# One lasting PSUM tile for attention scores and transposes, with two sets of columns for the transposes

## The chip, the cores and the metric

The kernel runs on one core of a Trainium2 chip. The metric is the device time of one execution in microseconds (us); the kernel before was run three times. One further execution was recorded by the hardware profiler, and all traces here come from such executions. PE is the matmul engine (PEld its weight loads), DVE the vector engine, ACT the scalar engine, POOL the general one, and SP issues DMAs.

## The reference

One layer of a hybrid encoder on a sequence of 2048 tokens of width 1024: an RMS norm feeds one input projection; half of its outputs go through a diagonal complex state-space scan (SSM) with a gated unit, the other half through chunked attention; both are normalised, joined by an output projection and a residual, and followed by a SwiGLU feed-forward block and a last norm. The part that matters here, cut:

```python
# 8 heads of 64; a chunk of 64 queries sees its own and the 8 previous chunks (BAND = 576 keys)
scores = jnp.einsum('bnqhd,bnkhd->bhnqk', qc, kb) / math.sqrt(HEAD_DIM)
scores = scores + bias[None, :, None, :, :]
scores = jnp.where(valid[None, None, :, None, :], scores, -1e30)
probs = jax.nn.softmax(scores, axis=-1)
out = jnp.einsum('bhnqk,bnkhd->bnqhd', probs.astype(v.dtype), vb)
```

## The kernel before

The kernel writes fp32 products as sums of two or three products of rounded parts: a `hi` part (a copy by ACT) and a `lo` part (the rest, by DVE). Matmul operands come from SBUF; results go to PSUM, of which a partition has eight pieces (banks) of 512 fp32 columns.

`att_phase` (about 130 to 740 us of the profiled execution) walks through 128 steps. A step is one block of 512 tokens (`sb`, four of them), one pair of heads (`pr`, four), one head of the pair (`hh`) and one group of 128 queries (`qp`, four). In step `s` the kernel emits, in the order `"sptf"`:

- **s, `scores(s)`**: the scores of 128 queries against `nk` keys, 640 in blocks 1 to 3, and 128, 256, 384 and 512 in the first block. They are the matmuls `sc<-k,q2h` and `sc<-k,q2l` (L79, a helper that records all matmuls), into the tile `sc` of two banks. 640 keys are done as 2 x 320 columns, one half in each bank. Then DVE adds the bias and takes the minimum in one pass (L849, two rows in the trace: the pass `s<-sc` and the read-out of the minimum, `mn`), and ACT does the exponential (L852, `s<-s,mn`).
- **p, `pv_head` and `pv_scale`**: every fourth step the product of a finished head's probabilities with v (16 matmuls `pj<-pth,v` and `pj<-ptl,v`, 8 in the first block), and every eighth step four transposes that spread the softmax sums.
- **t, `transp(s - 2)`**: up to five 128 x 128 transposes of the exponentials of two steps earlier (L82, `pt<-ident,s`) into the tile `pt` (five blocks of 128 columns, two banks); then ACT copies them to `pth` (L867) and DVE writes the rest to `ptl` (L868).
- **f**: the fillers, which are slices of other work spread over the steps by `Unit`: projections of later blocks (`pf`), v, and the SSM groups (`pj<-U,Bst` and others), whose scan POOL does.

With `PINA` set, all of these matmuls and transposes are kept in program order on PE. A scheduler orders the other engines and derives the semaphore waits from the accesses to each tile. `sc` and `pt` are allocated anew in every step, each with one buffer, so the next step's tile waits until the readers of the last one are through. PSUM in this phase holds two banks for `pf`, two for `pj`, two for `pt` and two for `sc`. From step 119 on the SSM buffers are given back and the mixing phase (the gated unit, then the output projection) begins among the last steps; after it come the feed-forward phases, which the change does not touch.

Of the kernel before, what the change touches and what calls it, by code (L numbers as in the profile page):

```python
# [13 lines left out]
ALU = mybir.AluOpType  # L14
AX = mybir.AxisListType

P = 128
# [9 lines left out]
SB = 512  # L27
# [69 lines left out]
def f32(ap):  # L97
    return ap.bitcast(F32)
# [302 lines left out]
def u_phase(k, ident, S, aw):  # L401
# [3 lines left out]
    with ExitStack() as cx:  # L405
# [113 lines left out]
        for n in range(1, NSB):  # L519
            last, b = BLOCKS[n - 1 : n + 1]  # L520
            prep(b)
            if n == 1:
                bias_corners(k, S["nba"])
                bias_rows(k, S, 0, S["nba"])
            pf = FBANKS[n]
            now = [group(b, 0, 0 in pf)]
            finish(last, held)
            long(1)
            if n == NSB - 1:
                att = att_phase(k, ident, S, aw, X[b], lambda: ST[b])  # L530
                next(att)
            for f in (1, 2):
                now.append(group(b, f, f in pf))
                if n > 1:
                    long(1)
            sums(b)
            held = now + [group(b, 3, 3 in pf)]
# [140 lines left out]
def att_phase(k, ident, S, aw, x0, roots):  # L678

    tc, nc, io, pfs = k.tc, k.nc, k.io, k.pfs  # L680
    with ExitStack() as cx:
# [138 lines left out]
        def load_nb(h):  # L820
            return bias_rows(k, S, h, nbt[h % 2])

        def scores(st):
            sb, pr, hh, qp = st
            h = 2 * pr + hh
            if qp == 0:
                hd = st_head[sb, h] = Head()
                hd.nb = nbs.pop(h) if nbs else load_nb(h)
                hd.s = {}
                hd.p = None  # L830
            hd = st_head[sb, h]
            if qp == 2 and (sb, h) < (NSB - 1, H - 1):
                nbs[(h + 1) % H] = load_nb((h + 1) % H)
            q2h, q2l, k2 = qk[sb, pr][hh]
            k0 = max(qp, 4) if sb == 0 else qp
            nk = (qp + 5 - k0) * P
            half = nk // 2 if nk > 512 else nk
            nch = nk // half
            ps = k.t(psum2, "sc", [P, 2, 512])
            for c in range(nch):  # L840
                c0 = k0 * P + c * half + k2.shape[1] - 2 * SB
                cols = slice(c0, c0 + half)
                for n, q2 in ((0, q2h), (1, q2l)):
                    k.ta.matmul(ps[:, c, :half], q2[:, qp * P : (qp + 1) * P], k2[:, cols], start=n == 0, stop=n == 1)
            s = k.t(aa, "s", [P, 640], bufs=3)
            mn = k.t(aa, "mn", [P, 1], bufs=4)
            if (hh, qp) == (0, 0):
                sums[sb, pr] = k.t(aa, "sm", [P, 2, 4], bufs=3)
            nc.vector.tensor_tensor_reduce(  # L849
                s[:, :nk].rearrange("p (a b) -> p a b", a=nch), ps[:, :nch, :half],  # L850
                hd.nb[:, nk - 1 :: -1].rearrange("p (a b) -> p a b", a=nch), 1.0, 3e38, ALU.add, ALU.min, mn[:])
            nc.scalar.activation(s[:, :nk], s[:, :nk], AF.Exp, bias=mn[:], scale=-1.0, accum_out=sums[sb, pr][:, hh, qp : qp + 1])  # L852
            hd.s[qp] = s, k0

        def transp(st):
            sb, pr, hh, qp = st
            hd = st_head[sb, 2 * pr + hh]
            if qp == 0:
                hd.p = k.t(aa, "pth", [P, 5, 4, P], F32R), k.t(aa, "ptl", [P, 5, 4, P], F32R)
            pth, ptl = hd.p  # L860
            s, k0 = hd.s.pop(qp)
            pt = k.t(psum, "pt", [P, 5, P], bufs=1)
            for kb in range(k0, qp + 5):
                k.ta.transpose(pt[:, kb % 5, :], s[:, (kb - k0) * P : (kb - k0 + 1) * P], ident[:])
            runs = [(0, 5)] if sb else ([(4, 5)] if qp == 0 else [(4, 5), (0, qp)])
            for a, b in runs:
                nc.scalar.copy(pth[:, a:b, qp, :], pt[:, a:b, :])  # L867
                nc.vector.tensor_tensor(ptl[:, a:b, qp, :], pt[:, a:b, :], f32(pth[:, a:b, qp, :]), op=ALU.subtract)  # L868
# [54 lines left out]
        sp = tc.alloc_tile_pool(name="ssm", reuse_waits="tile", bufs=1)  # L923
        psum = cx.enter_context(tc.tile_pool(name="aps", bufs=1, space=bass.MemoryType.PSUM, reuse_waits="tile"))
        psum2 = cx.enter_context(tc.tile_pool(name="aps2", bufs=1, space=bass.MemoryType.PSUM, reuse_waits="tile"))
        units = []
        for sb in range(NSB):
            g0 = sb * 32
# [12 lines left out]
        for s in range(N + LAG + 2):  # L941
            if s == OPEN:
                aw.release()
                mix = mix_phase(k, S, lambda: k.t(pfs, "pf", [P, 512]))
                units += [Unit(islice(mix, MIX_N), MIX_N, GSTART, N + LAG, GSTART - OPEN)]
            if s == GSTART:
                sp.release()
            for o in ORDER:
                if o == "s" and s < N:
                    scores(steps[s])  # L950
                elif o == "t" and LAG <= s < N + LAG:
                    transp(steps[s - LAG])
                elif o == "p" and LAG + 1 <= s < N + LAG + 1 and steps[s - LAG - 1][3] == 3:
                    pv_head(steps[s - LAG - 1])
                elif o == "p" and s >= LAG + 2 and steps[s - LAG - 2][2:] == (1, 3):
                    pv_scale(steps[s - LAG - 2])
                elif o == "f":
                    for u in units:
                        u.advance(s)
# [737 lines left out]
```

## Time and profile before

| | |
|---|---|
| runs | 2290.89, 2288.25, 2294.39 us; median 2290.89 |
| profiled execution | 2289.1 us, span 2287.1 us |
| PE busy | 2171.6 us (95%), 10632 matmuls and transposes |
| DVE, ACT, POOL busy | 1544.7 (68%), 1000.6 (44%), 348.7 us (15%) |
| granted PE clock, mean | 0.978 |

Busy time is the time in which an engine had an instruction under way. A row of the trace names the line, the engine, the operation, the tile written and those read, and their shapes. A releaser (`<-`) is the instruction whose semaphore ended an engine's idle time. Matmul ends are modelled.

### The profile page before, as it was taken

What the parts mean: (1) busy time and instruction counts of PE and PEld (TensorE: products, weight loads), DVE (VectorE), ACT (ScalarE), POOL (GpSimd) and SP (SyncE); (2) the same over time, 40 slices, a digit from 0 to 9 for tenths busy, and PEclk for the clock granted to TensorE, in tenths of its full rate; (3) what the DMA queues carried; (4) which work ended last, traced back from release to release, by engine and by line L of the source; (5) the groups of instructions that cost most, each with busy time, mean ns of one, the idle gap of its engine ahead of it and who ended that gap; (6) DMA issues with size and microseconds to landing.
All of it is one profiled execution on the core that took longest, in us unless ns stands there. A gap on an engine that the chain in (4) does not pass through costs nothing.

```text
span 2287.1 us, 30278 instructions
## 1 busy us (share of the span) xinstructions
PE 2171.6 (95%) x10632; PEld 1830.1 (80%) x10632; DVE 1544.7 (68%) x2695; ACT 1000.6 (44%) x1654; POOL 348.7 (15%) x813
## 2 busy tenths in 40 slices
PE   8988899999996899999999999999999989999997
PEld 6777688898985788878888887888888778888886
DVE  7755565555556766876776678666666477789776
ACT  6444555455557652343333335333333343344322
POOL 2245765455660000000000000000000000000000
PEclk9998999999998999999999999999999999999999
DMA  8767886666644534854465567555423297465552
GB/s 299 236 221 220 257 223 201 187 188 179 188 132 124 171 121 147 267 189 151 160 200 178 167 211 258 203 169 188 139 96 110 78 341 252 166 212 193 206 189 74
DMA packets 215256, 428.33 MB, mean 187 GB/s; under 512 B 38592, under 2 KB 61168, under 8 KB 208000
## 3 DMA queue, kind: packets, MB, share of 16 engines
q1 hardware_dynamic: 210368, 412.50, 55.3%
q0 software_dynamic: 4736, 13.91, 2.0%
q8 instruction: 83, 1.36, 0.2%
q14 instruction: 69, 0.57, 0.1%
HBM read 286.86 MB, written 129.00 MB: 182 GB/s over the span
## 4 chain that ended last, share of the span: by engine, by line
PE 80%; DVE 6%; DMA 4%; POOL 4%; issue 3%; ACT 1%; SPq 1%; DVEq 0%; POOLq 0%; ACTq 0%
PE X L79 20%; PE ps L79 19%; PE Y L79 10%; PE pf L79 9%; PE big L79 9%; PE W L79 5%; PE pj L79 4%; PE sc L79 2%; PE pt L82 2%; DMA xt<-in_xp 1%; DMA hd<-wc 1%; POOL X L605 1%; DVE lo L156 1%; POOL X L604 1%; POOL st L602 1%
## 5 line engine op out<-in xcount | busy, mean ns | idle before, releaser
L79 PE MATMUL X<-hi,c 128*128 128x512 f32 x1408 | 451.0, 391 | 6.9 <-DVE c L156 5.4
L79 PE MATMUL ps<-hd,hd 128*128 128x512 f32 (+1 forms) x1968 | 430.8, 381 | 6.1 <-ACT hd L156 4.5
L79 PEld LDWEIGHTS ps<-hd,hd 128*128 128x128 f32 x1968 | 358.0, 189 | 77.7 <-ACT hd L156 5.3
L79 PEld LDWEIGHTS X<-hi,c 128*128 128x128 f32 x1408 | 265.3, 189 | 63.4 <-DVE c L156 6.3
L79 PE MATMUL X<-lo,c 128*128 128x512 f32 x704 | 274.9, 391 | 0.0
L156 ACT CAST hd<-hd 128x1536 fp32r<-128x1536 f32 (+1 forms) x106 | 147.7, 1393 | 236.3 <-DMA hd<-hq 178.7
L79 PE MATMUL Y<-hi,c 128*128 128x512 f32 x704 | 224.7, 390 | 1.5 <-DVE u L1389 1.5
L156 DVE TENSOR_TENSOR hd<-hd 128x1536 fp32r<-128x1536 f32 (+1 forms) x106 | 174.4, 1646 | 29.1 <-ACT hd L156 28.4
L156 DVE TENSOR_TENSOR c<-S,c 128x512 fp32r<-128x512 f32 x176 | 121.0, 689 | 98.3 <-ACT c L156 98.0
L1385 ACT COPY u<-X 128x512 f32<-128x512 f32 x132 | 77.4, 587 | 200.7 <-PE X L79 200.7
L1513 DVE TENSOR_TENSOR acc<-acc,ps 128x512 f32<-128x512 f32 x196 | 130.9, 684 | 50.3 <-PE ps L79 47.8
L156 ACT CAST c<-S 128x512 fp32r<-128x512 f32 x176 | 109.4, 622 | 120.1 <-PE Y L79 61.6
L79 PE MATMUL pf<-hi,w 128*128 128x512 f32 x416 | 153.9, 422 | 8.4 <-ACT w L156 4.7
L79 PE MATMUL big<-m,woh 128*128 128x512 f32 x512 | 161.2, 396 | 0.0
L79 PEld LDWEIGHTS Y<-hi,c 128*128 128x128 f32 x704 | 132.5, 188 | 29.9 <-DVE u L1389 2.2
L79 PEld LDWEIGHTS X<-lo,c 128*128 128x128 f32 x704 | 132.8, 189 | 27.5
L156 ACT CAST c<-raw 128x512 fp32r<-128x512 f32 x132 | 82.3, 623 | 150.5 <-PE Y L79 68.5
L79 PE MATMUL Y<-lo,c 128*128 128x512 f32 x352 | 137.2, 390 | 0.0
L868 DVE TENSOR_TENSOR ptl<-pt,pth 128x640 fp32r<-128x640 f32 (+3 forms) x152 | 98.3, 647 | 47.5 <-ACT pth L867 45.9
L852 ACT ACTIVATE s<-s,mn 128x640 f32<-128x640 f32 (+4 forms) x128 | 98.0, 765 | 65.6 <-DVE mn L849 61.1
L867 ACT CAST pth<-pt 128x640 fp32r<-128x640 f32 (+3 forms) x152 | 83.8, 551 | 95.6 <-PE pt L82 91.5
L79 PE MATMUL W<-hi,c 128*128 128x512 f32 x352 | 115.5, 389 | 0.0
(441 smaller groups left out, 4169.9 us busy)
## 6 DMA issues: line engine op xcount, KB each, us to landing
w<-wss SPq DMA_DIRECT2D x36, 1024.0 KB, 6.0
hq<-g SPq DMA_DIRECT2D x140, 256.0 KB, 2.1
hd<-hq SPq DMA_DIRECT2D x42, 768.0 KB, 4.5
hd<-wc SPq DMA_DIRECT2D x42, 768.0 KB, 6.0
raw<-in_w_gate SPq DMA_DIRECT2D x44, 512.0 KB, 3.8
raw<-in_w_up SPq DMA_DIRECT2D x44, 512.0 KB, 4.3
wc<-px SPq DMA_DIRECT2D x66, 256.0 KB, 3.2
wss<-w SPq DMA_DIRECT2D x12, 1024.0 KB, 5.7
```

Of the source, the lines that this page charges most:

```text
L79: return self.tc.keep_in_program_order(self.tc.nc.tensor.matmul(*a, **b))
L82: return self.tc.keep_in_program_order(self.tc.nc.tensor.transpose(*a, **b))
L156: return nc.scalar.copy(hi, raw), nc.vector.tensor_tensor(lo, raw, f32(hi), op=ALU.subtract)
L602: eng.tensor_tensor(t[:, :, :, :n], src, ar, op=ALU.mult)
L604: eng.tensor_tensor(dst, dst, t[:, :, :, :n], op=ALU.add)
L605: eng.tensor_tensor(dst, dst, t2[:, :, :, :n], op=ALU.add)
L852: nc.scalar.activation(s[:, :nk], s[:, :nk], AF.Exp, bias=mn[:], scale=-1.0, accum_out=sums[sb, pr][:, hh, qp : qp + 1])
L867: nc.scalar.copy(pth[:, a:b, qp, :], pt[:, a:b, :])
L868: nc.vector.tensor_tensor(ptl[:, a:b, qp, :], pt[:, a:b, :], f32(pth[:, a:b, qp, :]), op=ALU.subtract)
L1385: nc.scalar.copy(u[:], ps[:])
L1513: V.tensor_tensor(a, a, ps[:], op=ALU.add)
```

## The change

`sc` and `pt` go. One tile `ring` of 2048 columns (four banks) is allocated once, ahead of the steps, and all scores and transposes use parts of it:

- columns 0 to 639: transposes of even `qp`; columns 640 to 1279: transposes of odd `qp`;
- scores up to 384 wide: from column 1536 on; wider ones (512 and 640) get 256 columns in front, 1280 to 1535, as a matmul pair of their own, and the rest from 1536 on.

In terms of banks of 512 columns, the even transposes lie in banks 0 and 1, the odd ones in 1 and 2, the front piece of the scores in bank 2 and the rest in bank 3. The DVE pass reads the scores as one run of columns.

```diff
-            half = nk // 2 if nk > 512 else nk
-            nch = nk // half
-            ps = k.t(psum2, "sc", [P, 2, 512])
-            for c in range(nch):
-                c0 = k0 * P + c * half + k2.shape[1] - 2 * SB
-                cols = slice(c0, c0 + half)
-                for n, q2 in ((0, q2h), (1, q2l)):
-                    k.ta.matmul(ps[:, c, :half], q2[:, qp * P : (qp + 1) * P], k2[:, cols], start=n == 0, stop=n == 1)
+            head = 256 if nk > 384 else 0
+            ps = ring[:, 1536 - head : 1536 - head + nk]
+            for a, b in ((0, head), (head, nk)):
+                if a < b:
+                    c0 = k0 * P + k2.shape[1] - 2 * SB
+                    for n, q2 in ((0, q2h), (1, q2l)):
+                        k.ta.matmul(ps[:, a:b], q2[:, qp * P : (qp + 1) * P], k2[:, c0 + a : c0 + b], start=n == 0, stop=n == 1)
...
-            nc.vector.tensor_tensor_reduce(
-                s[:, :nk].rearrange("p (a b) -> p a b", a=nch), ps[:, :nch, :half],
-                hd.nb[:, nk - 1 :: -1].rearrange("p (a b) -> p a b", a=nch), 1.0, 3e38, ALU.add, ALU.min, mn[:])
+            nc.vector.tensor_tensor_reduce(s[:, :nk], ps, hd.nb[:, nk - 1 :: -1], 1.0, 3e38, ALU.add, ALU.min, mn[:])
...
-            pt = k.t(psum, "pt", [P, 5, P], bufs=1)
+            pt = ring[:, 640 * (qp % 2) : 640 * (qp % 2) + 640].rearrange("p (a b) -> p a b", a=5)
...
+        ring = k.t(psum2, "ring", [P, 2048])
```

## The prediction

> **What bounds the kernel now.** I read the page first (busy time, slices, chain), then the attention stretch by windows, then what PE waits for there, and last the timeline of single steps. A row of the windows gives the stretch, its length, the busy time and instructions of PE, PEld, DVE, ACT and POOL, the granted clock, the DMA share and GB/s.
>
> ```profile
> PE 2171.6 (95%) x10632; PEld 1830.1 (80%) x10632; DVE 1544.7 (68%) x2695; ACT 1000.6 (44%) x1654; POOL 348.7 (15%) x813
> PE 80%; DVE 6%; DMA 4%; POOL 4%; issue 3%; ACT 1%; SPq 1%; DVEq 0%; POOLq 0%; ACTq 0%
> 130.00:282.00 152.00, 124.24 (x673) 106.48 (x674) 83.33 (x191) 75.64 (x189) 88.88 (x197) 0.90 0.76 233
> 282.00:685.00 403.00, 384.03 (x2370) 349.53 (x2369) 229.36 (x402) 217.53 (x436) 218.26 (x527) 0.97 0.66 187
> 685.00:740.00 55.00, 38.05 (x202) 31.45 (x201) 32.08 (x67) 37.57 (x56) 1.04 (x2) 0.84 0.44 130
> ```
>
> PE is 95% busy and holds 80% of the chain that ended last. The three windows cover the 128 attention steps (32 in the first, 87 in the second, 9 in the third). In the middle one PE is busy for 384 of 403 us, DVE for 229, ACT for 218: PE alone is the bound, and its instructions of this stretch stand in a fixed order. So whatever makes PE stand still there moves everything behind it, unless PE would have stood still later anyway; that is 27.8 + 19.0 + 17.0 = 64 us in the three windows.
>
> **What the change does to the waits.** The arithmetic hardly moves. What moves is who waits for whom. Before, scores and transposes had a tile each: the scores of a step waited until DVE had read the last step's scores, its transposes until DVE had written the last step's `ptl`. Now both live in one tile that is never given back, and the built program shows what follows: in each of the 126 steps that have scores and transposes, the first transpose waits for the DVE instruction that reads the scores issued just ahead of it in the same step, with the even set of columns as with the odd one; and in 122 steps the scores wait for `ptl` of the step just before. The two sets of columns are thus not used as two: the waits are those of the whole tile.
>
> **The first wait, step by step.** One step with a free DVE, and one with the hop back to PE:
>
> ```profile
> 443.20 0.31 PE L79 MATMUL sc<-k,q2l 128*128 128x320 f32 x1
> 443.35 0.71 PE L82 MATMUL pt<-ident,s 128*128 128x128 f32 x5
> 443.55 0.82 DVE L849 CUSTOM_DVE_ANT_0 s<-sc,nba 128x640 f32<-128x640 f32 x1 [1.49 <-PE sc L79]
> 444.30 0.08 DVE L849 DVE_READ_ACCUMULATOR2_ANT mn<- 128x1 f32 x1
> ...
> 686.81 0.08 DVE L849 DVE_READ_ACCUMULATOR2_ANT mn<- 128x1 f32 x1
> 686.95 0.42 PE L79 MATMUL sc<-k,q2h 128*128 128x320 f32 x1 [1.11 <-DVE mn L849]
> ...
> 437.62 0.71 PE L82 MATMUL pt<-ident,s 128*128 128x128 f32 x5
> 437.98 0.81 DVE L849 CUSTOM_DVE_ANT_0 s<-sc,nba 128x640 f32<-128x640 f32 x1
> 438.71 0.08 DVE L849 DVE_READ_ACCUMULATOR2_ANT mn<- 128x1 f32 x1
> ```
>
> Today the transposes start at 443.35, behind the last scores and beside the DVE pass over them. From now on they start after that pass has ended (444.38) and the semaphore has come back (686.89 to 686.95: 0.06), at 444.44: 1.09 us later. In the second step DVE comes from another instruction and PE would start at 438.85 instead of 437.62: 1.23. Where DVE is later still, its delay is PE's too. I take 1.2 between the two, since DVE is sometimes later than in either. Behind the waiting transpose stand the step's fillers (projection, SSM, v), all of PE's other work; ACT's `pth` and DVE's `ptl` wait for the transposes. Nothing on PE can pass.
>
> Steps in which something lies between scores and transposes pay less:
>
> ```profile
> 448.45 0.08 DVE L849 DVE_READ_ACCUMULATOR2_ANT mn<- 128x1 f32 x1
> 449.86 0.73 PE L82 MATMUL pt<-ident,s 128*128 128x128 f32 x5
> ...
> 484.64 0.71 PE L82 MATMUL pt<-ident,s 128*128 128x128 f32 x5
> 485.16 0.08 DVE L849 DVE_READ_ACCUMULATOR2_ANT mn<- 128x1 f32 x1
> ...
> L849 DVE CUSTOM_DVE_ANT_0 s<-sc,nba 128x512 f32<-128x512 f32 x4 | 2.8, 692 | 3.3 <-PE sc L79 3.3
> L849 DVE CUSTOM_DVE_ANT_0 s<-sc,nba 128x384 f32<-128x384 f32 x4 | 2.2, 558 | 3.8 <-PE sc L79 3.7
> L849 DVE CUSTOM_DVE_ANT_0 s<-sc,nba 128x256 f32<-128x256 f32 x4 | 1.7, 424 | 7.1 <-PE sc L79 7.1
> L849 DVE CUSTOM_DVE_ANT_0 s<-sc,nba 128x128 f32<-128x128 f32 x4 | 1.2, 290 | 4.4 <-PE sc L79 4.1 <-DMA nba<-nbs 0.4
> ```
>
> With the 16 matmuls of `pv_head` between (every fourth step) the DVE pass is over 1.33 us before the transposes: nothing to pay. With the four transposes of `pv_scale` (every eighth) it ends at 485.24, +0.06, against 484.64: 0.66. In the first block of 32 steps the scores are 128 to 512 wide, and the pass takes 0.29 to 0.69, mean 0.49, instead of 0.82: 0.33 less. The sum: 60 plain steps of 640 columns x 1.2 = 72; 12 with `pv_scale` x 0.7 = 8; 20 plain ones of the first block x 0.87 = 17, 3 more there with `pv_scale` x 0.4 = 1; 31 with `pv_head` x 0. Together 98 us.
>
> **The second wait.** The scores of the next step wait for `ptl`. What leads there (stretch 282 to 685, the last rows from the timeline):
>
> ```profile
> L868 DVE TENSOR_TENSOR ptl<-pt,pth 128x640 fp32r<-128x640 f32 x85 | 70.0, 824 | 27.4 <-ACT pth L867 26.2
> L867 ACT CAST pth<-pt 128x640 fp32r<-128x640 f32 x85 | 59.0, 694 | 59.7 <-PE pt L82 58.4
> ...
> 438.96 0.83 ACT L852 ACTIVATE s<-s,mn 128x640 f32<-128x640 f32 x1
> 439.69 0.19 ACT L852 ACTIVATION_READ_ACCUMULATOR s<-s,mn 128x1 f32 x1
> ...
> 487.28 0.31 PE L79 MATMUL sc<-k,q2h 128*128 128x320 f32 x1
> ...
> 566.60 0.71 PE L82 MATMUL pt<-ident,s 128*128 128x128 f32 x5
> 568.53 0.31 PE L79 MATMUL sc<-k,q2h 128*128 128x320 f32 x1
> ```
>
> In the built program ACT now does the exponential of the step first, then `pth`. After the end of the DVE pass (438.79) ACT is free at 439.88, 1.09 later; then `pth` 0.69, `ptl` 0.82 and two hops, 0.1: the scores may start 2.7 after the pass. PE, started again 0.06 after it, needs 2.64 with nine fillers (484.64 to 487.28): 2.70, no wait. With six (566.60 to 568.53) it needs 1.99: 0.7 of waiting. I count 15 such short steps in the timeline, ten of them behind `pv_head`, where the exponential is done early and the wait is some 0.5: 3.5 + 5 = 8. The last steps from 685 on have no fillers at all and pay 1 to 2 each, 5 in all. Together 13; from 5 (ACT takes `pth` first) to 25 (DVE's other work gets between). Gross: 98 + 13 = 111 us.
>
> **What takes some of it back.** Waits of PE, by window (160 to 282, then 282 to 700, then from 700), for what does not come from PE's last step:
>
> ```profile
> PE pj L79 <- DMA XG<-X: 3.6, 2, 1.9
> PE pj L79 <- DMA Tm<-kts: 1.5, 1, 1.5
> ...
> PE pj L79 <- DMA Tm<-kts: 9.7, 3, 3.7
> PE pj L79 <- DMA XG<-X: 1.9, 1, 1.9
> ...
> PE pf L79 <- ACT gh L156: 6.8, 1, 6.8
> ...
> PE pt L82 <- DVE ptl L868: 14.7, 7, 3.8
> POOL st L602 <- ACT X L588: 217.3, 8, 32.6
> ```
>
> A later PE finds the SSM loads there: 16.7 us of DMA waits, of which I take 13, because each load is issued two or three steps earlier and these steps grow by over 2 us. Of the 6.8 at the start of the mixing 4; the half-clock windows behind such waits that go with them, 2. That is 19. The POOL scans do not become the bound: POOL waits 217 us for PE's and ACT's SSM products and only gets them later. SP's queue keeps its order; its loads wait for readers on PE and so stay in step with it. The old wait for `ptl`, 14.7 us, is not a gain: it moves to the next scores.
>
> **Edits at nothing.** 2 x 320 columns become 256 + 384 with the same two weight loads each; the rows above run at one matmul per 0.15 us (443.20 to 443.35) for 320 columns, and columns are the same in sum. Eight steps of 512 columns get one more pair, under 0.1 us each, below 1 us together. The DVE pass reads 640 columns in one piece instead of two: same count, 0.82 either way, between -0.02 and +0.02 us x 96 = 2 us, and on the path now. No DMA is added or moved.
>
> **Sum.** 111 - 19 = 92 on the profiled execution's 2289.1 us (its span is 2287.1): 2381. The median of the runs is 1.8 higher, so 2383.
>
> **Rivals.** (1) *The clock falls.* The stalls come every 4 to 5 us, and the granted clock does fall after idle stretches:
>
> ```profile
> 390.64:394.05 3.41, 1.32 (x8) 0.88 (x6) 3.35 (x7) 3.41 (x8) 3.02 (x10) 0.99 0.76 260
> 394.05:397.47 3.42, 3.42 (x12) 3.02 (x13) 2.89 (x5) 2.14 (x5) 3.08 (x13) 0.51 0.87 326
> 243.80:247.20 3.40, 1.57 (x10) 1.43 (x11) 2.23 (x4) 1.65 (x4) 3.24 (x6) 1.00 0.96 352
> ```
>
> A window with 1.32 us busy (39%) was followed by one at 0.51; the one with 1.57 (46%) kept 1.00. A plain step with its 1.2 us of idle leaves 2.2 of 3.41 us, 65%; a short one, 1.9 of idle, 44%, at the edge. So few windows should fall. If one in five of the 118 in the middle stretch did, 24 x 3.4 x half x two thirds busy = 27 us: 2410; with more, 2430. [...] Chance 0.11.
>
> (2) *Only shared banks cost.* The odd set's last 256 columns (1024 to 1279) lie in the same 512-column piece as the first 256 of the scores; the even set shares nothing with them. If only odd steps paid, that is half of 98, and without the second wait in even steps: +45, 2336. [...] The waits of the built program speak against it; 0.03.
>
> (3) *It does what two sets promise, and is faster.* If the transposes no longer waited for the last `ptl` and the new waits were met in time, the 14.7 us and the score wait of 1.11 shown at 686.95 would go: 2275. It decides where the DVE pass has ended when the scores have; it ends 1.03 after the transposes' old start in the best step shown. 0.03.
>
> (4) *No change,* 2291: PE's new stalls fall wholly into the 64 us that it idles anyway and the rest is won by the freed `ptl` wait. 64 is less than 111, and only a part of it is waiting for others: 0.02.
>
> **How the numbers follow.** Forecast 0.81. Its bounds: 1.09 instead of 1.2 (-7), second wait 5 (-8), 32 of the 64 us taken back (-13), below that a part of (2): 2345. Above: nothing taken back (+19), second wait 25 (+12), half of (1) (+14): 2428. Slower by over 0.3% (7 us, about what these runs can tell from no change: they spread over 6) holds the forecast, (1) and (2): 0.95; faster 0.03; same 0.02.
>
> **What would show it.** Right: PE's waits name "pt <- DVE mn" first, some 80 to 100 us over about 95 times; the L849 pass (L848 now) stays at 0.82; the matmul counts and durations outside attention stay; the 282 to 685 stretch grows by about 70 to 75 us; everything from the mixing on keeps its length. Wrong in part: clock below 0.95 in the attention stretch (rival 1); stalls in every second step only (2). Wrong altogether: "pt" with waits no longer than today's 14.7 us, or a shorter attention stretch.

## The result

The changed kernel takes 2390.1 us (median of four runs, 2388.3 to 2391.5), the kernel before 2291.4 us (four runs, 2288.3 to 2294.4): a ratio of 1.0433, 95% interval 1.0415 to 1.0451. It is slower by 99 us. The profiled execution has a span of 2389.8 us, 102.7 more than before, and a mean granted clock of 0.974 (0.978 before).

### The profile page after: what moved, and what is told of

The parts are those of the page before. It is cut to its first block, busy times and chain, and to the rows that moved or that the text cites. A ratio compares the mean times of both kernels' runs of the same rounds, so it can differ in the third digit from the quotient of the medians.

```text
span 2389.8 us, 30314 instructions
## 1 busy us (share of the span) xinstructions
PE 2204.9 (92%) x10648; PEld 1831.8 (77%) x10648; DVE 1545.4 (65%) x2695; ACT 1005.5 (42%) x1654; POOL 340.0 (14%) x813
## 4 chain that ended last, share of the span: by engine, by line
PE 78%; DVE 7%; DMA 4%; ACT 3%; issue 3%; SPq 2%; DVEq 0%; ACTq 0%
PE X L79 19%; PE ps L79 19%; PE Y L79 10%; PE pf L79 9%; PE big L79 8%; PE W L79 5%; PE pj L79 3%; PE ring L82 2%; PE ring L79 2%; DVE s L848 2%; SPq L564 1%; DVE ptl L865 1%; DMA xt<-in_xt 1%; ACT pth L864 1%; SPq L649 0%
## 5 line engine op out<-in xcount | busy, mean ns | idle before, releaser
L79 PE MATMUL X<-hi,c 128*128 128x512 f32 x1408 | 451.8, 392 | 7.0 <-DVE c L156 5.0
L79 PE MATMUL ps<-hd,hd 128*128 128x512 f32 (+1 forms) x1968 | 432.9, 382 | 5.7 <-DVE hd L156 4.0
L79 PEld LDWEIGHTS ps<-hd,hd 128*128 128x128 f32 x1968 | 359.6, 190 | 77.7 <-DVE hd L156 5.1
L79 PEld LDWEIGHTS X<-hi,c 128*128 128x128 f32 x1408 | 265.8, 189 | 64.0 <-DVE c L156 5.8
L79 PE MATMUL X<-lo,c 128*128 128x512 f32 x704 | 275.2, 391 | 0.0
L79 PE MATMUL Y<-hi,c 128*128 128x512 f32 x704 | 225.0, 390 | 1.6 <-DVE u L1387 1.6
L82 PE MATMUL ring<-ident,s 128*128 128x128 f32 x560 | 90.5, 290 | 85.7 <-DVE mn L848 84.8
L865 DVE TENSOR_TENSOR ptl<-ring,pth 128x640 fp32r<-128x640 f32 (+3 forms) x152 | 98.4, 647 | 109.3 <-ACT pth L864 107.9
L79 PE MATMUL big<-m,woh 128*128 128x512 f32 x512 | 163.1, 400 | 0.0
L79 PE MATMUL pf<-hi,w 128*128 128x512 f32 x416 | 152.5, 419 | 3.8 <-ACT w L156 3.5
L79 PEld LDWEIGHTS Y<-hi,c 128*128 128x128 f32 x704 | 132.6, 188 | 30.1 <-DVE u L1387 2.5
L79 PEld LDWEIGHTS X<-lo,c 128*128 128x128 f32 x704 | 133.0, 189 | 27.5
L82 PEld LDWEIGHTS ring<-ident,s 128*128 128x128 f32 x560 | 61.7, 145 | 111.9 <-DVE mn L848 58.1
L79 PE MATMUL Y<-lo,c 128*128 128x512 f32 x352 | 137.2, 390 | 0.0
```

What stands on the lines that cost most here:

```text
L79: return self.tc.keep_in_program_order(self.tc.nc.tensor.matmul(*a, **b))
L82: return self.tc.keep_in_program_order(self.tc.nc.tensor.transpose(*a, **b))
```

## The profile after

The page of the changed kernel, the engines' busy time and the shares of the chain that ended last:

```profile
PE 2204.9 (92%) x10648; PEld 1831.8 (77%) x10648; DVE 1545.4 (65%) x2695; ACT 1005.5 (42%) x1654; POOL 340.0 (14%) x813
PE 78%; DVE 7%; DMA 4%; ACT 3%; issue 3%; SPq 2%; DVEq 0%; ACTq 0%
```

DVE and ACT do what they did before (1544.7 and 1000.6 us). PE is down from 95 to 92%. POOL has left the chain, and DVE and ACT have gained a point or two in it.

The windows of the changed kernel, cut where the first block, the middle 87 steps and the last steps now lie, and the rest of the kernel behind the last step's scores:

```profile
130.00:300.00 170.00, 133.11 (x697) 111.49 (x698) 90.21 (x198) 78.91 (x193) 88.14 (x197) 0.89 0.70 220
300.70:770.50 469.80, 394.43 (x2354) 337.47 (x2353) 221.98 (x395) 218.84 (x431) 211.27 (x528) 0.99 0.56 157
770.50:836.00 65.50, 44.24 (x202) 34.67 (x201) 32.18 (x66) 37.59 (x55) 0.00 (x0) 0.77 0.35 105
826.80:2389.80 1563.00, 1523.50 (x6832) 1261.33 (x6830) 1106.57 (x1751) 609.48 (x873) 0.00 (x0) 0.98 0.53 177
```

And the kernel before, cut at the same steps (scores of step 32 to scores of step 119, then from the last step's scores on):

```profile
284.60:684.50 399.90, 380.93 (x2354) 346.87 (x2353) 229.36 (x402) 216.68 (x434) 218.05 (x526) 0.97 0.65 187
...
731.30:2287.00 1555.70, 1517.36 (x6832) 1256.96 (x6830) 1107.05 (x1751) 610.44 (x873) 0.00 (x0) 0.99 0.52 178
```

The middle stretch has the same 2354 PE instructions and takes 469.8 us instead of 399.9: +69.9. PE is idle for 75.4 us of it instead of 19.0 (+56.4) and busy 13.5 longer; the clock is no lower (0.99 against 0.97). By the starts of the scores in the two traces, the first 32 steps grow from 152.2 to 168.5 us (+16.3), the steps from 119 on from 46.7 to 56.2 (+9.5), and everything behind them from 1555.8 to 1563.0 (+7.2). These four make up the 102.7, less 0.2 by which the attention begins earlier.

What PE waits for in the attention (changed kernel, 130 to 860 us; the columns are us in total, times, longest):

```profile
PE ring L82 <- DVE mn L848: 84.8, 94, 2.9
PE ring L79 <- DVE ptl L865: 22.1, 32, 2.7
PE pf L79 <- ACT gh L156: 6.8, 1, 6.8
...
PE pj L79 <- DMA Tm<-kts: 3.7, 2, 3.2
```

The two waits that head the list are new. The first is that of the transposes (L82) for the read-out of the pass over the scores just issued; the second is that of the scores (L79) for `ptl`. The wait `pt <- DVE ptl` (14.7 us before) is gone, as are the waits for `XG`; those for `Tm` are shorter.

One plain step of the changed kernel and the end of a step with `pv_head` and six fillers, from the timeline (in brackets the idle time ahead of the row and what ended it):

```profile
501.59 0.28 PE L79 MATMUL ring<-k,q2h 128*128 128x256 f32 x1
...
502.01 0.33 PE L79 MATMUL ring<-k,q2l 128*128 128x384 f32 x1
502.38 0.82 DVE L848 CUSTOM_DVE_ANT_0 s<-ring,nbb 128x640 f32<-128x640 f32 x1 [1.81 <-DMA nba<-nbs]
503.13 0.08 DVE L848 DVE_READ_ACCUMULATOR2_ANT mn<- 128x1 f32 x1
503.36 0.74 PE L82 MATMUL ring<-ident,s 128*128 128x128 f32 x5 [1.02 <-DVE mn L848]
506.01 0.28 PE L79 MATMUL ring<-k,q2h 128*128 128x256 f32 x1
...
512.68 0.08 DVE L848 DVE_READ_ACCUMULATOR2_ANT mn<- 128x1 f32 x1
514.23 0.73 PE L82 MATMUL ring<-ident,s 128*128 128x128 f32 x5
515.78 0.82 DVE L865 TENSOR_TENSOR ptl<-ring,pth 128x640 fp32r<-128x640 f32 x1
516.66 0.38 PE L79 MATMUL ring<-k,q2h 128*128 128x256 f32 x1 [0.30 <-DVE ptl L865]
```

The plain step takes 4.42 us (501.59 to 506.01); the same step took 3.20 before: +1.22. Of this 1.02 is the wait shown, and most of the rest is overlap: before, the first transpose began 0.16 ahead of the modelled end of the last scores, now 1.02 behind it. Over the middle stretch this lost overlap, by estimate 0.16 us at each of the 82 waits there (65 of the first kind, 17 of the second), makes up 13 of the 13.5 us by which PE is busy longer. Behind `pv_head` the pass is over 1.47 us before the transposes (512.76 to 514.23) and costs nothing; but with only six fillers the next scores wait for `ptl` (0.30, and 0.16 of overlap lost, as above).

## The experiments

The theory: PE stands still because the tile, not the columns, is what a transpose or a score waits for; the sharing of one tile is the whole cost, as a wait for the own step's pass and a wait for the last step's `ptl`. Rivals: that the other edits (lasting tile, 256 + 384, the pass in one piece) cost something; that only shared banks cost; that a lower clock does.

**Scores and transposes in two tiles.** Everything else of the change stays, but one set of columns:

```diff
-            ps = ring[:, 1536 - head : 1536 - head + nk]
+            ps = scs[:, 512 - head : 512 - head + nk]
...
-            pt = ring[:, 640 * (qp % 2) : 640 * (qp % 2) + 640].rearrange("p (a b) -> p a b", a=5)
+            pt = pts[:, :640].rearrange("p (a b) -> p a b", a=5)
...
-        ring = k.t(psum2, "ring", [P, 2048])
+        scs = k.t(psum2, "scs", [P, 1024])
+        pts = k.t(psum, "pts", [P, 1024])
```

> The changed kernel with its one lasting tile cut in two: the scores keep 256 + 384 columns and the one-piece DVE pass in a lasting tile of two banks of their own, the transposes use one set of columns in another lasting tile of two banks. Theory (PE waits inside the step because scores and transposes are parts of one tile): the waits are those of the kernel before, so 2291 us, within 8. Rival (the lasting allocation, the 256 + 384 split or the one-piece pass costs the time): about 2390.

Measured: 2292.0 us, ratio 1.0007 (0.9988 to 1.0025). Its waits of PE:

```profile
PE pts L82 <- DVE ptl L865: 12.9, 7, 3.3
PE pj L79 <- DMA Tm<-kts: 11.5, 4, 4.6
```

These are the waits of the kernel before (14.7 and, for `Tm`, 1.5 + 9.7). So the lasting tile, the split and the one-piece pass cost nothing that these runs can tell (the interval reaches from -3 to +6 us), and the 99 us are the price of one tile for both.

**One set of columns, still one tile.** All transposes go to columns 0 to 639, two banks that the scores never touch:

```diff
-            pt = ring[:, 640 * (qp % 2) : 640 * (qp % 2) + 640].rearrange("p (a b) -> p a b", a=5)
+            pt = ring[:, :640].rearrange("p (a b) -> p a b", a=5)
```

> The changed kernel with all transposes in columns 0 to 639, so that transposes lie in the first two banks and scores in the last two, still in one tile. Theory (the waits are those of the whole tile, the second set changes nothing): 2390 us, within 6, with the same 85 us of PE waits for the DVE pass. Rival (only a bank that both use makes them wait): no wait left between them, about 2291.

Measured: 2391.5 us, ratio 1.0428 (1.0403 to 1.0453); PE's first wait:

```profile
PE ring L82 <- DVE mn L848: 86.3, 94, 4.3
```

The same 94 waits although no bank is shared: rival (2) falls. The second set of columns neither costs nor brings anything. This kernel and the one with two tiles both have one set of columns and differ in the tile alone: 2391.5 against 2292.0 us.

**The pass twice**, in the changed kernel and in the kernel before, to see where it lies on the path:

```diff
-            nc.vector.tensor_tensor_reduce(s[:, :nk], ps, hd.nb[:, nk - 1 :: -1], 1.0, 3e38, ALU.add, ALU.min, mn[:])
+            for _ in range(2):
+                nc.vector.tensor_tensor_reduce(s[:, :nk], ps, hd.nb[:, nk - 1 :: -1], 1.0, 3e38, ALU.add, ALU.min, mn[:])
```

> The changed kernel with the DVE pass over the scores done twice (the result is the same). Theory (PE stands still until that pass has ended): each plain full-width step pays another 0.85 us, 60 x 0.85 = 51, the 12 steps with pv_scale 10, the first block 12, the steps with pv_head nothing: 73 more, 2463 us, between 2450 and 2490. Rival (the loss is elsewhere, the pass is hidden as before): under 10 more, as in the kernel before.

> The kernel before with the DVE pass over the scores done twice. Theory: the pass lies beside PE's fillers, DVE is busy for some 307 instead of 229 us of the 403 us from 282 to 685, and PE does not wait for it: 2291 to 2306 us. Rival (the pass is on PE's path there too): about 2365.

Measured: the kernel before goes to 2303.3 us (ratio 1.0048, 1.0023 to 1.0072), within what was expected: but for some 11 us the second pass is hidden there. The changed kernel goes to 2543.8 us (ratio 1.1098, 1.1063 to 1.1132), 154 us over the changed kernel with one pass, where 73 were expected. Its first wait of PE, the 87 steps of its middle stretch, and single windows of 3.41 us in pairs, each with the one that follows:

```profile
PE ring L82 <- DVE mn L849: 188.2, 99, 5.0
```

```profile
319.00:916.10 597.10, 453.64 (x2355) 387.54 (x2353) 290.11 (x564) 219.91 (x431) 207.75 (x528) 0.88 0.44 124
...
458.15:461.56 3.41, 1.53 (x10) 1.11 (x9) 1.67 (x4) 0.34 (x1) 3.10 (x7) 1.00 0.98 293
461.56:464.98 3.42, 3.42 (x12) 2.83 (x11) 0.82 (x1) 1.28 (x3) 3.11 (x11) 0.50 0.03 10
888.23:891.64 3.41, 1.58 (x13) 1.25 (x11) 2.17 (x5) 1.16 (x3) 3.30 (x5) 1.00 0.61 178
891.64:895.06 3.42, 3.42 (x18) 2.80 (x16) 0.82 (x1) 0.36 (x1) 3.02 (x4) 1.00 0.54 139
```

The wait grew by 103 us, not by 73: some 85 of it are the second pass and its read-out (0.82 + 0.08) in the 94 steps that waited before; the other 18 were not traced to steps. The rest, some 50 us, goes with the clock: 0.88 in the middle stretch against 0.99, and PE is busy there for 453.6 us instead of 394.4 with the same work. A window in which PE was busy for 1.53 of 3.41 us (45%) was followed by one at half clock, one with 1.58 (46%) was not. Of the 40 windows at full clock from 322 to 915 us that were followed by half clock 35 were busy for 45% or less; only one that low was not. The limit is not sharp: of 19 windows between 46 and 53% five were followed by half clock. This is rival (1)'s mechanism, at twice the dose. In the changed kernel from 322 to 770 us the windows, but for one, do not get that empty:

```profile
431.31:434.72 3.41, 1.88 (x9) 1.18 (x8) 3.35 (x7) 3.35 (x7) 3.02 (x6) 1.00 0.66 194
601.97:605.38 3.41, 1.17 (x6) 0.61 (x4) 3.35 (x5) 2.22 (x5) 1.54 (x3) 1.00 0.87 205
605.38:608.80 3.42, 3.03 (x10) 2.65 (x11) 1.85 (x4) 1.61 (x3) 0.00 (x0) 0.50 0.98 268
```

Of its 132 windows from 322 to 770 us the emptiest is the one at 601.97, busy for 34%, and it is the only one with a drop behind it. The next emptiest, at 431.31, is at 55%. The clock's 50 us are read from the windows; no run took the clock alone.

**Each wait alone.** Two tiles, and a matmul of one element (`ones` by `ones`) that takes on one of the waits: into the scores' tile ahead of the transposes, so that it waits for the own step's pass, or into the transposes' tile ahead of the scores, so that it waits for the last `ptl`. A third run has the same small matmul right behind the scores, where it waits for nothing new, to price it.

```diff
# first wait alone, in transp
+            k.ta.matmul(scs[:1, :1], k.ones[:], k.ones[:], start=True, stop=True)
# second wait alone, in scores
+            k.ta.matmul(pts[:1, 1023:], k.ones[:], k.ones[:], start=True, stop=True)
# no wait: in scores, behind the scores' own matmuls
+            k.ta.matmul(scs[:1, :1], k.ones[:], k.ones[:], start=True, stop=True)
```

> Scores and transposes in two lasting tiles as in two_tiles, and ahead of each step's transposes a matmul of one element into the scores' tile (an unused column). It waits for the DVE pass over this step's scores, so the first wait of the changed kernel is there without the second. Theory: 98 us of stalls less 19 that PE's other waits take back, 79, and under 0.1 us for each extra matmul, some 5: 2375 us, between 2360 and 2385. Rival (the two waits only cost together, as one chain): under 2330.

> The same two tiles, and ahead of each step's scores a matmul of one element into the transposes' tile (an unused column). It waits for ptl of the step before: the second wait without the first. Theory: 13 us, of which 5 in the steps without fillers from 685 us on, and some 5 for the extra matmuls: 2305 us, between 2296 and 2315. Rival (this wait carries the loss): over 2340.

> Two tiles, and the same small matmul as in the two runs with one wait each, now issued right behind the scores' own matmuls into the scores' tile, so that it waits for nothing new; 128 of them. Theory: the small matmul has a price of its own on PE, about 0.15 us by the rows of the runs that held it, 128 x 0.15 = 19 us over the kernel before: about 2311 us (2300 to 2318). Taken off the two earlier runs, the wait for the step's own pass is then worth about 72 us and the wait for the read-out of the previous step about 22, in sum about the change's 99. Rival: the small matmul is free (under 4 us, about 2294): then the second wait alone is worth 41 us and the two waits overlap in the change.

Measured: 2385.2 us with the first wait, ratio 1.0399 (1.0372 to 1.0425); 2336.9 with the second, 1.0183 (1.0156 to 1.0209); 2311.6 with the small matmul alone, 1.0086 (1.0056 to 1.0116). By the ratios the first two lost 91 and 42 us, where 84 and 18 were expected. The small matmul isn't free: it costs 0.0086 x 2291 = 20 us (13 to 27 by the interval), not 5, which is 15 of the difference in each. PE's first wait in the first and in the second of these kernels, and the group of small matmuls in the third (300 to 690 us), a fence for each:

```profile
PE scs L79 <- DVE mn L848: 89.4, 95, 2.0
```

```profile
PE pts L79 <- DVE ptl L866: 34.5, 36, 3.9
```

```profile
L79 PE MATMUL scs<-ones 128*1 128x1 f32 x162 | 15.3, 164 | 0.0
```

With that taken off, on the assumption that the small matmul costs the same in all three kernels, the first wait is worth (0.0399 - 0.0086) x 2291 = 72 us and the second (0.0183 - 0.0086) x 2291 = 22 us, each give or take some 9 by the intervals, where 79 and 13 were expected. Together they are 94, and the change costs 99: within the intervals the two waits add up to the whole.

**Half of the fillers between scores and transposes**, in the changed kernel, so that PE has work while the pass runs:

```diff
-ORDER = "sptf"
+ORDER = "sphtf"
...
+        if half:
+            want = self.done + (want - self.done) // 2
```

> The changed kernel with the fillers of a step cut in two: the smaller half is issued between scores and transposes (ahead of pv_head), the rest behind the transposes. With both waits in one tile a step is one chain: scores 0.76, DVE pass and hop 1.1, transposes 0.73, pth 0.74, ptl and hop 0.9, 4.2 us, whatever PE has to do beside it. A plain step with nine fillers takes 4.4 now and gains 0.2 at most, the steps with 12 to 24 fillers (4.5 to 5.3) up to 1 each: 15 to 30 us in all, 2360 to 2375. Rival (PE only lacks cover for the DVE pass): most of the 85 us of that wait goes, about 2310.

Measured: 2372.8 us, ratio 1.0344 (1.0317 to 1.0370). The waits and one step:

```profile
PE ring L79 <- DVE ptl L867: 66.3, 96, 2.9
PE ring L82 <- DVE mn L850: 20.1, 46, 2.3
```

```profile
502.78 0.38 PE L79 MATMUL ring<-k,q2h 128*128 128x256 f32 x1 [0.99 <-DVE ptl L867]
...
503.67 0.82 DVE L850 CUSTOM_DVE_ANT_0 s<-ring,nbb 128x640 f32<-128x640 f32 x1 [0.23 <-PE ring L79]
...
504.54 0.83 ACT L851 ACTIVATE s<-s,mn 128x640 f32<-128x640 f32 x1 [0.49 <-DVE mn L850]
504.56 0.76 PE L82 MATMUL ring<-ident,s 128*128 128x128 f32 x5 [0.23 <-DVE mn L850]
...
505.28 0.19 ACT L851 ACTIVATION_READ_ACCUMULATOR s<-s,mn 128x1 f32 x1
...
505.49 0.69 ACT L866 CAST pth<-ring 128x640 fp32r<-128x640 f32 x1
...
506.22 0.82 DVE L867 TENSOR_TENSOR ptl<-ring,pth 128x640 fp32r<-128x640 f32 x1 [0.52 <-ACT pth L866]
...
507.10 0.39 PE L79 MATMUL ring<-k,q2h 128*128 128x256 f32 x1 [0.37 <-DVE ptl L867]
```

PE now waits little for the pass (20.1 us instead of 84.8), but the wait turns up at the next scores (66.3 instead of 22.1). The rows show why: scores, pass, transposes, `pth`, `ptl`, scores are one chain around the tile, 4.32 us long (502.78 to 507.10), and moving the fillers takes nothing out of it. Beside the transposes stands ACT's exponential of the same step, which also begins when the pass has ended; in this step it is the later of the two (505.47 against 505.32), and `pth` follows it at 505.49. With two tiles the scores no longer wait for `ptl` nor the transposes for the pass, so that there is no such chain. None of these kernels beats the kernel before; the one with two tiles equals it.

## Why the prediction was right, and where it was off

The forecast case came true by its own mechanism; the time was 2390 against 2383.

- *The first wait.* Right in kind and size: 84.8 us over 94 times (80 to 100 over about 95 forecast), and with the 0.16 of overlap lost each time some 100 us of delay, where the sum had 98. By class, plain steps of the middle stretch grew by 1.22 (median of 54; forecast 1.2), those with `pv_scale` by 0.81 (0.7), those with `pv_head` and enough fillers by 0.01 (0). Alone it costs 72 us net. The tile, not the columns, is the unit of waiting, which the built program said and the run with one set showed.
- *The middle stretch* grew by 69.9 us (70 to 75 forecast); the L848 pass took 0.82 as before. The waits came with no bank shared as well: 94 of them, 86.3 us, in the run with one set.
- *The second wait* came to 22.1 us. The sum had 13 for it and let the old wait for `ptl`, 14.7, move to the next scores beside that. Of the seven old waits six turn up at the scores of their steps (12, 21, 28, 59, 123 and 124), with 8.1 us; the other 6.6 went away, which was not forecast. New are 14.1, near the 13, but spread otherwise: 5.5 in the middle (8 forecast; the steps behind `pv_head` that pay grew by 0.46, forecast 0.5), 4.0 in the last steps (5), and 4.6 in the first block, where the sum had no term. The first block's waits, old and new, up to 300.7 us:

```profile
PE ring L82 <- DVE mn L848: 15.3, 22, 2.1
PE ring L79 <- DVE ptl L865: 9.0, 10, 2.7
```

- *What is taken back* was too much by 8 us, 11 instead of 19. The loads were indeed met later. The 16.7 us of DMA waits were 14.7 (one of 1.9 for `XG` lies across the cut at 282 us and stood in both windows); 3.7 for `Tm` are left, so 11 of the 13 forecast came back. The 4 us at the start of the mixing did not come: `pf <- ACT gh` stayed at 6.8. Nor did the 2 us of clock: the last nine steps had 0.77 instead of 0.84.
- *Everything from the mixing on keeps its length* was wrong by 7 us: 1563.0 against 1555.7, PE busy 6.1 longer. The clock accounts for most of it, by estimate: the clock records have half clock there for 47.0 us instead of 32.8, with PE busy for 31.4 of them instead of 20.0, and half of the 11.4 between these is 5.7. It need not be the change's doing. In the ten kernels, which run the same code there, the stretch took 1555.8 to 1565.2 us with 32.8 to 49.5 us at half clock; the one with two tiles, whose waits are those of the kernel before, has 1559.5 and 43.3. Why the time at half clock differs was not settled.
- *The sum.* The profiled execution grew by 102.7 us, where the sum had 92. It misses both ways: the 8 us that were not taken back and the 7 from the mixing on made it too low, the 6.6 of old waits that went away too high. That these offset each other in part is luck; the 98 of the first wait is not.
- *The clock* (rival 1) stayed at 0.99 in the middle stretch. The sign named for this rival, below 0.95 in the attention, could not tell: over all steps the kernel before has 0.94 (130 to 740 us) and the changed one 0.94 too (130 to 836 us). What the forecast's two windows showed, half clock behind 39% and none behind 46%, held in the changed kernel from 322 to 770 us (half clock behind the window at 34%, none behind those from 55% up); in its first block windows at 51 and 48% (243.57 and 277.71 us) were followed by half clock too. With the pass done twice half clock came behind nearly all windows with 1.9 us of idle or more; in the changed kernel from 322 to 770 us it did not come behind windows with up to 1.5.
- *Rivals (3) and (4)* needed waits that are met in time; 94 were not.

## What to carry to other kernels

Where a scheduler tracks a tile as one thing, two uses of one tile make their readers wait for each other, whatever columns they use (2391.5 us here, against 2292.0 with a tile each): give each use a tile of its own before giving it a second set of columns. Look in the built program for what each first write waits for, then read in the timeline how long ago that was over at the point where the engine gets there; the difference, step class by step class, is the price. If work moved into such a gap only moves the wait (here from 84.8 to 20.1 us at the transposes, but from 22.1 to 66.3 at the scores), the gap belongs to a chain that is longer than the step, and the chain has to be cut.

## What the hardware showed that was not expected

- The granted clock fell behind single windows of 3.41 us by how busy PE was in them (in the attention of the changed kernel the trace has half clock in stretches of 3.41, 6.83, 10.24 and 20.48 us). With the pass done twice it fell nearly always at 45% and below (35 of 36 windows) and now and then at up to 52% (five of 19 between 46 and 53%), without any long idle gap: one wait of 1.88 us sufficed at 458 us, and between 322 and 915 us, where 40 windows were followed by half clock, the longest gap was 3.06.
- A matmul of one element is not free: it appears as two instructions of 0.16 us, one behind the other (162 for 81 steps), and cost 20 us (13 to 27) over 128 steps, 0.15 us a step.
